# The w_out half of a squared-ReLU MLP: products carried through all of h in four passes, with the left-hand sums made a stage earlier

## The chip, the cores and the metric

The kernel runs on one core of a Trainium2 chip. The metric is the device time of one execution in microseconds (us). The engines are called as the profile calls them: PE (TensorE, matmuls; PEld its weight loads), DVE (VectorE), ACT (ScalarE), POOL (GpSimd) and SP (SyncE, which issues most DMAs).

## The reference

Two decoder layers over 1024 tokens of width 1024, in float32. Both end in the same kind of MLP, with a hidden width of 4096; the mixers and the shared K/V projection between the layers are not touched by the change.

```python
def sq_relu_mlp(h, w_in, w_out):
    return jnp.square(jax.nn.relu(h @ w_in)) @ w_out
...
for layer in range(DEPTH):
    ...                      # layer 0: RWKV-7 time mixing; layer 1: forgetting attention
    x = x + sq_relu_mlp(rmsnorm(x, mlp_norm_g[layer]), mlp_w_in[layer], mlp_w_out[layer])
    if layer == N_A_LAYERS - 1:
        k_sh, v_sh, c_sh = shared_kv(x, kv_norm_g, kv_w, kv_f_bias, k_norm_g)
```

## The kernel before, in words

Each layer's MLP has two stages. `mlp_in` (the w_in stage) computes h = relu(x w_in)^2 and stores it to DRAM; `mlp_out` (the w_out stage) loads it again and adds h w_out to the residual stream, which stays in SBUF as `xt`, eight tiles of 128 tokens by 1024.

Both stages multiply blocks of 2 by 2 quarters with seven products in place of eight. The left operands are four quarters or sums of them (A11, A12, A22, S1 = A21 + A22, S2 = S1 - A11, S3 = A11 - A21, S4 = A12 - S2), the right ones likewise (B11, B21, B22, T1 = B12 - B11, T2 = B22 - T1, T3 = B22 - B12, T4 = B21 - T2). Each result quarter is a sum of some products; U and V hold partial sums that several quarters share. The list SEVEN pairs them: (A11, B11), (A12, B21), (S2, T2), (S1, T1), (S3, T3), (A22, T4), (S4, B22).

Every operand is split into two parts of a reduced float32 type that PE takes at full rate (`split`): the high part is a cast, mostly on ACT (L700), the low part is source minus high part, a TENSOR_TENSOR on DVE or POOL (L703). A product of two split operands is three matmuls: high by high, high by low, low by high (L736 to L738 in w_in, L1329 to L1331 in w_out). A matmul here is 128x128 by 128x512.

`mlp_in` goes over 16 pairs of 128-column tiles of w_in (one tile from each half of the 4096 columns). A pair loads 1 MB of w_in, makes four sums of it on DVE (`form`, L1185), splits seven operands (`ah`, `al`; the low parts alternate between POOL and DVE), does seven products of twelve matmuls, and collects each with an add from PSUM on DVE (L1193). The four quarters of the pair's h get ReLU on ACT (L1195) and their square as a product on POOL (L1196). `z` holds h of a pair; two DMAs of 512 KB store it to `d_H`, on SP's queue, for the last pair on POOL's.

`mlp_out` calls `add_product`, which goes over the 4096 rows of w_out in four chunks. A chunk loads eight tiles of h and eight of w_out (tile `r`, 512 KB each), makes left-hand sums (S) and right-hand sums (T) on tiles of 128x512 by DVE and POOL, splits both sides (`oh`, `ol`), and does seven products of 48 matmuls, each into four PSUM banks. After each product of each chunk, DVE adds the banks to `xt` or to U (L1342); in the last chunk U is added to three quarters of `xt`, twelve of these adds on POOL (L1347). The result goes out on SP's queue (L1361): to `d_x` in layer 0, to `out` in layer 1.

Which engine an operation goes to is read from tables of letters (ENG, ENG_O). The order on each engine is set by a scheduler that simulates the program, with priority for some parts (`high_priority`); matmuls issued through `k.pe` and some loads are kept in program order. Memory is given out by pools whose order on the stack is a list of names, so a tile of one stage can wait for the last reader of a tile of the stage before.

## Time and profile before

| | us |
|---|---|
| three runs | 2941.09, 2938.45, 2939.36 (median 2939.36) |
| profiled execution | 2935.41 |
| its span | 2933.7, mean granted clock 0.947 |
| w_in, layer 0 | 890.6 to 1205.4 |
| w_out, layer 0 | 1205.4 to 1575.4 |
| w_in, layer 1 | 2250.3 to 2569.6 |
| w_out, layer 1 | 2569.6 to 2929.7 |

The stage borders are PE's: from the first matmul of a w_in stage to its last, from there to the last matmul of w_out. A few matmuls of layer 0's w_in (48 of 1344) stand before its row. "Granted clock" is the share of full speed that PE had. In groups of instructions a row reads: line, engine, operation, output and inputs, shapes, count, then busy time and mean ns of one, then the idle time of the engine just before them and what ended it. In a timeline a row has its start, its duration, and in brackets the idle time before it with its releaser.

### The profile page before, as it was taken

Reading aid. Unit: us, or ns where it says so; the run is one execution under the profiler, and the core shown is the slowest. Engines: PE = TensorE matmul, PEld = TensorE weight load, DVE = VectorE, ACT = ScalarE, POOL = GpSimd, SP = SyncE. Lnnn points to the kernel's source line nnn. Section 1 sums busy time; section 2 is a strip of 40 time slices with the busy share of each in tenths; the row PEclk is TensorE's granted clock in tenths of the full one; section 3 lists DMA queues with packets and bytes.
Section 4 is the critical chain, followed back from the end, with each engine's and each line's share of the span. In section 5 each row is a group of like instructions: output and inputs, shape, how many; then the busy total and the mean of one; then the engine's idle time right before and its main releaser. Section 6 shows DMA issues by size and latency. Waiting matters only on the chain.

```text
span 2933.7 us, 47183 instructions
## 1 busy us (share of the span) xinstructions
PE 2637.7 (90%) x17922; PEld 2183.9 (74%) x17922; DVE 2254.4 (77%) x3497; ACT 1191.8 (41%) x2245; POOL 1471.8 (50%) x1054
## 2 busy tenths in 40 slices
PE   7997788789998999889987899899986999989998
PEld 4776686677776888667766899888865888867876
DVE  7049998777768555699998878587789755599998
ACT  6364433432244333323334434487735333322432
POOL 3055553475546554566664422324266555466555
PEclk9998888899998999999998899999998999999999
DMA  3358574655412333532202232554330333442311
GB/s 116 141 180 247 159 210 137 176 164 145 116 50 72 115 111 105 201 115 100 73 11 92 72 102 75 164 148 134 95 123 13 97 114 108 143 159 86 115 58 58
DMA packets 330867, 344.66 MB, mean 117 GB/s; under 512 B 137392, under 2 KB 257440, under 8 KB 330640
## 3 DMA queue, kind: packets, MB, share of 16 engines
q1 hardware_dynamic: 329648, 339.48, 37.0%
q8 instruction: 141, 2.31, 0.3%
q0 software_dynamic: 992, 2.17, 0.2%
q14 instruction: 86, 0.70, 0.1%
HBM read 236.59 MB, written 104.99 MB: 116 GB/s over the span
## 4 chain that ended last, share of the span: by engine, by line
PE 50%; DVE 23%; issue 5%; DMA 3%; POOL 3%; ACT 1%; SPq 0%; DVEq 0%; POOLq 0%; ACTq 0%
PE mm L354 8%; PE mm L738 7%; PE mm L737 7%; PE mm L736 7%; DVE ol L703 5%; PE mm L1330 4%; PE mm L1331 4%; PE mm L1329 3%; DVE xt L1342 3%; PE wo L354 2%; PE tp L357 2%; PE o L354 1%; DVE Tm L301 1%; PE s L354 1%; DVE Tb L303 1%
## 5 line engine op out<-in xcount | busy, mean ns | idle before, releaser
L1330 PE MATMUL mm<-ol,oh 128*128 128x512 f32 x992 | 402.3, 408 | 43.9 <-DVE ol L703 38.5
L1331 PE MATMUL mm<-oh,ol 128*128 128x512 f32 x992 | 385.3, 405 | 16.1 <-DVE ol L703 15.7
L1329 PE MATMUL mm<-oh 128*128 128x512 f32 x992 | 365.7, 401 | 29.3 <-ACT oh L700 20.4
L1330 PEld LDWEIGHTS mm<-ol,oh 128*128 128x128 f32 x992 | 194.9, 197 | 100.5 <-DVE ol L703 52.6
L1329 PEld LDWEIGHTS mm<-oh 128*128 128x128 f32 x992 | 191.5, 194 | 76.6 <-ACT oh L700 23.2
L1196 POOL TENSOR_TENSOR z<-z 128x512 f32<-128x512 f32 x128 | 144.0, 1126 | 205.4 <-ACT z L1195 203.0
L1331 PEld LDWEIGHTS mm<-oh,ol 128*128 128x128 f32 x992 | 193.1, 196 | 63.3 <-DVE ol L703 23.2
L700 ACT CAST oh<-r 128x512 fp32r<-128x512 f32 x211 | 124.0, 619 | 250.1 <-PE mm L1330 192.8
L737 PE MATMUL mm<-xlT,ah 128*128 128x512 f32 x512 | 203.6, 398 | 17.1 <-DVE xlT L703 16.9
L736 PE MATMUL mm<-xhT,ah 128*128 128x512 f32 x512 | 202.1, 396 | 7.7 <-ACT xhT L700 5.5
L738 PE MATMUL mm<-xhT,al 128*128 128x512 f32 x512 | 202.0, 395 | 0.0
L703 DVE TENSOR_TENSOR ol<-r,oh 128x512 fp32r<-128x512 f32 x193 | 189.3, 1009 | 6.5 <-ACT oh L700 3.8
L1342 DVE TENSOR_TENSOR xt<-xt,mm 128x512 f32<-128x512 f32 x288 | 181.4, 675 | 7.0 <-PE mm L1331 6.9
L700 ACT CAST ah<-w 128x512 fp32r<-128x512 f32 x125 | 77.4, 621 | 182.5 <-PE mm L737 175.5
L703 POOL TENSOR_TENSOR ol<-r,oh 128x512 fp32r<-128x512 f32 x63 | 99.3, 1580 | 97.0 <-ACT oh L700 81.7
L738 PE MATMUL mm<-xhB,al 128*128 128x512 f32 x368 | 143.5, 391 | 1.0 <-DVE al L703 1.0
L737 PE MATMUL mm<-xlB,ah 128*128 128x512 f32 x368 | 144.1, 392 | 0.0
L736 PE MATMUL mm<-xhB,ah 128*128 128x512 f32 x368 | 143.9, 391 | 0.0
L700 ACT CAST oh<-S 128x512 fp32r<-128x512 f32 x102 | 63.0, 622 | 187.2 <-PE mm L1330 144.7
L737 PEld LDWEIGHTS mm<-xlT,ah 128*128 128x128 f32 x512 | 98.1, 192 | 41.4 <-DVE xlT L703 20.3
L703 DVE TENSOR_TENSOR ol<-S,oh 128x512 fp32r<-128x512 f32 x102 | 111.5, 1097 | 17.7 <-ACT oh L700 13.5
L703 POOL TENSOR_TENSOR ol<-T,oh 128x512 fp32r<-128x512 f32 x58 | 93.7, 1618 | 52.3 <-ACT oh L700 33.4
(527 smaller groups left out, 7794.5 us busy)
## 6 DMA issues: line engine op xcount, KB each, us to landing
w<-in_mlp_w_in_dram SPq DMA_DIRECT2D x64, 512.0 KB
r<-d_H SPq DMA_DIRECT2D x64, 512.0 KB
r<-in_mlp_w_out_dram SPq DMA_DIRECT2D x64, 512.0 KB
d_H<-z SPq DMA_DIRECT2D x60, 512.0 KB
raw<-in_rwkv_w_rkv_dram SPq DMA_DIRECT2D x24, 512.0 KB
d_KR<-KR SPq DMA_DIRECT2D x16, 512.0 KB
KRz<-d_KR SPq DMA_DIRECT2D x16, 512.0 KB
KRz<-d_BK SPq DMA_DIRECT2D x16, 512.0 KB
```

The lines of the kernel that those rows point to most:

```text
L354: return self.tc.keep_in_program_order(self.tc.nc.tensor.matmul(*args, **kw))
L357: return self.tc.keep_in_program_order(self.tc.nc.tensor.transpose(*args))
L700: nc.scalar.copy(hi, src)
L703: lo_eng.tensor_tensor(lo, src, hi.bitcast(F32), op=ALU.subtract)
L736: te.matmul(out, ah, bh, start=i == 0, stop=False)
L737: te.matmul(out, ah, bl, start=False, stop=False)
L738: te.matmul(out, al, bh, start=False, stop=i == n - 1)
L1196: nc.gpsimd.tensor_tensor(dst, dst, dst, op=ALU.mult)
L1329: te.matmul(banks[t], ah[:, ts], bh, start=i == 0, stop=False)
L1330: te.matmul(banks[t], ah[:, ts], bl, start=False, stop=False)
L1331: te.matmul(banks[t], al[:, ts], bh, start=False, stop=i == n - 1)
L1342: nc.vector.tensor_tensor(d, d, o, op=ALU.add)
```

## The change

`mlp_in`:

- The seven products of a pair come in another order (IN_ORDER), with A22 last.
- The square is made on ACT (Relu, then Square) instead of POOL. The low parts of w_in's operands are all on DVE (from the third pair on; before, every other one was on POOL).
- DVE makes the left-hand sums of h for w_out, four TENSOR_TENSORs of 128x512 a pair. S3 takes the place of C12 in `z`; S1, S2 and S4 go to new tiles `sums`.
- All seven left operands are stored: `d_H` has eight tiles of [128, 7, 2, 512], and a pair stores 7 x 256 KB in three DMAs on SP's queue, 29.4 MB a stage instead of 16.8.
- The split buffers go from four to three, and two operand pools change places in layer 1.

`mlp_out`:

- It goes over the 4096 rows four times, in passes of two products (the last of one): (A11, A12), (S2, S1), (S3, S4), (A22). A pass takes eight steps `q`; both products keep their four PSUM banks through all eight, and only then DVE adds them, 32 adds of 128x512 in a stage.
- A step loads its left operands ready made (`ra`, four buffers) and quarters of w_out (`rb`, six buffers, 256 rows of 512 columns, 2 KB each) on SP: 56 and 64 loads of 512 KB in a stage, 62.9 MB instead of 33.5.
- Right-hand sums and both parts of the split are made on tiles of 128x1024: high parts on ACT, low parts and sums on DVE. T2 is kept in SBUF for the last pass.
- POOL has twelve adds of U and V to `xt`, at the end of the second pass, and issues the stores of `d_x` and `out`.
- Matmuls are kept in program order. Their number stays 1344 a stage.

The K/V bias is loaded at the program's start, on POOL's queue.

The core of the diff:

```diff
--- before.py
+++ after.py
@@ -1145,6 +1147,11 @@
     return X
 
 
+IN_ORDER = ["A11", "A12", "S2", "S1", "S3", "S4", "A22"]
+
+LEFT = {n: i for i, n in enumerate(["A11", "S3", "A12", "A22", "S1", "S2", "S4"])}
+
+
 def mlp_in(k, a, l, xt, z, raw=None):
 
     nc, tc, ps = k.nc, k.tc, k.ps
@@ -1185,16 +1192,18 @@
                 engine(k, e).tensor_tensor(A[dst], A[x], A[y], op=op)
 
             def part(name, q, src=None):
-                S[name] = [wp.tile([P, NK // 2, P], F32R, tag=t, name=t, bufs=4) for t in ("ah", "al")]
-                es = [eng["wh"][7 * pr + q], eng["wl"][7 * pr + q]] if pr < 2 else ["s", "pv"[q % 2]]
+                S[name] = [wp.tile([P, NK // 2, P], F32R, tag=t, name=t, bufs=3) for t in ("ah", "al")]
+                es = [eng["wh"][7 * pr + q], eng["wl"][7 * pr + q]] if pr < 2 else ["s", "v"]
                 split(k, None, A[src or name], None, *(engine(k, e) for e in es), dst=S[name])
 
-            def add(dst, x, o, last=False):
+            def add(dst, x, o):
                 nc.vector.tensor_tensor(dst, x, o, op=ALU.add)
-                if last:
-                    nc.scalar.activation(dst, dst, AF.Relu)
-                    nc.gpsimd.tensor_tensor(dst, dst, dst, op=ALU.mult)
-            for q, (an, bn) in enumerate(SEVEN):
+
+            def square(x):
+                nc.scalar.activation(x, x, AF.Relu)
+                nc.scalar.activation(x, x, AF.Square)
+            for q, an in enumerate(IN_ORDER):
+                bn = dict(SEVEN)[an]
                 with tc.high_priority(offset=PRIO if pr == 0 or pr < AHEAD and q < 2 else 0):
                     if an == "S2":
                         A["S"] = wp.tile([P, NK // 2, P], F32, tag="S", name="S", bufs=1)
@@ -1221,21 +1230,33 @@
                     yield
                     Hs = z((pr + 1) % 2)
                     C11, C12, C21, C22 = Hs[:, 0, T1], Hs[:, 0, T2], Hs[:, 1, T1], Hs[:, 1, T2]
-                    add(C11, U, o, True)
+                    add(C11, U, o)
+                    square(C11)
                 elif an == "S2":
                     add(U, U, o)
                 elif an == "S1":
                     V = hp.tile([P, 512], F32, tag="V", name="V", bufs=1)
                     add(V, U, o)
                 elif an == "S3":
-                    add(C22, V, o, True)
+                    add(C22, V, o)
                     add(U, U, o)
-                elif an == "A22":
-                    add(C21, U, o, True)
+                    square(C22)
+                elif an == "S4":
+                    add(C12, V, o)
+                    square(C12)
+                    sums = [hp.tile([P, 2, 512], F32, tag="sums", name="sums") for _ in range(2)]
+                    (S1, S2), S4 = (sums[0][:, i] for i in range(2)), sums[1][:, 0]
+                    nc.vector.tensor_tensor(S1, C12, C22, op=ALU.add)
+                    nc.vector.tensor_tensor(S2, S1, C11, op=ALU.subtract)
+                    nc.vector.tensor_tensor(C12, C11, C12, op=ALU.subtract)
                 else:
-                    add(C12, V, o, True)
-            for h in range(2):
-                (nc.gpsimd if pr == F // 256 - 1 else nc.sync).dma_start(k.d_H[pr][:, h], Hs[:, h])
+                    add(C21, U, o)
+                    square(C21)
+                    nc.vector.tensor_tensor(S4, C21, S2, op=ALU.subtract)
+            dst = k.d_H[pr // 2][:, :, pr % 2]
+            nc.sync.dma_start(dst[:, 4:6], sums[0])
+            nc.sync.dma_start(dst[:, 0:4], Hs.rearrange("p h (f t) -> p (h f) t", t=512))
+            nc.sync.dma_start(dst[:, 6], S4)
         gens = [products(pr) for pr in range(F // 256)]
 
         def first_products(x):
@@ -1361,27 +1382,107 @@
                         nc.sync.dma_start(out[i * P:i * P + P, cols], d)
 
 
...
 def mlp_out(k, a, l, xt, out, norm):
 
-    nc, tc = k.nc, k.tc
+    nc, tc, ps = k.nc, k.tc, k.ps
+    w_out = a["mlp_w_out"][l]
+    D1, D2 = slice(0, 512), slice(512, 1024)
+    KP = F // 512
     with ExitStack() as ctx:
-        names = ("rb2-op-p-ra-rb1", "ra-op-p-rb1-rb2")[l].split("-")
+        names = ("k-ra-rb-op", "ra-rb-op-k")[l].split("-")
         p = {x: ctx.enter_context(tc.tile_pool(name="o_" + x, bufs=1, reuse_waits="tile")) for x in names}
-        raws = 0
-
-        def load(ap):
-            nonlocal raws
-            t = p[("ra", "rb1", "rb2")[raws % 24 // 8]].tile([P, 1024], F32, tag=f"r{raws % 24}", name=f"r{raws % 24}")
+        T2 = [p["k"].tile([P, 2, 512], F32, name=f"T2{i}") for i in range(KP)]
...
+        U, V = ([p["k"].tile([P, 512], F32, name=f"{n}{i}") for i in range(4)] for n in "UV")
+        SS = {}
+
+        def load(pool, n, ap):
+            t = p[pool].tile([P, 2, 512], F32, tag=pool, name=pool, bufs=n)
             with tc.high_priority(offset=PRIO):
                 tc.keep_in_program_order(nc.sync.dma_start(t, ap))
-            raws += 1
             return t
 
-        def tiles(c, h, i):
-            f = 4 * c + i
-            r0 = f * P + h * (F // 2)
-            return load(k.d_H[f][:, h]), load(a["mlp_w_out"][l][r0:r0 + P, :])
-        add_product(k, xt, F // P // 8, tiles, p["op"], p["p"], p["p"], out, norm, f"o{l}")
+        def left(name, q):
+            return load("ra", 4, k.d_H[q][:, LEFT[name]])
+
+        def right(name, q):
+            r0 = 256 * q + F // 2 * (name[1] == "2")
+            return load("rb", 6, w_out[r0:r0 + 256, (D1, D2)[int(name[2]) - 1]].rearrange("(j p) e -> p j e", p=P))
+
+        def parts(side, x):
+            h, lo = (p["op"].tile([P, 2, 512], F32R, tag=t + side, name="o" + t, bufs=3) for t in "hl")
+            return split(k, None, x, None, nc.scalar, nc.vector, dst=(h, lo))
+
+        def minus(dst, x, y):
+            nc.vector.tensor_tensor(dst, x, y, op=ALU.subtract)
+            return dst
+        quarter = {"11": lambda t: xt[t][:, D1], "12": lambda t: xt[t][:, D2],
+                   "21": lambda t: xt[t + 4][:, D1], "22": lambda t: xt[t + 4][:, D2]}
+        goes = {"A11": ["11"], "A12": ["11"], "S2": [], "S1": [], "S3": ["22", "21"], "S4": ["12"], "A22": ["21"]}
+        final = {"A12": "11", "S3": "22", "S4": "12", "A22": "21"}
+        for names in (("A11", "A12"), ("S2", "S1"), ("S3", "S4"), ("A22",)):
+            banks = {an: [ps.tile([P, 512], F32, tag="mm", name="mm") for _ in range(4)] for an in names}
+            for q in range(KP):
+                L = {an: left(an, q) for an in names}
+                if names[0] == "A11":
+                    R = {"A11": right("B11", q), "A12": right("B21", q)}
+                elif names[0] == "S2":
+                    b11, b12, b22 = (right(n, q) for n in ("B11", "B12", "B22"))
+                    t1 = minus(b12, b12, b11)
+                    R = {"S2": minus(T2[q], b22, t1), "S1": t1}
+                elif names[0] == "S3":
+                    b12, b22 = (right(n, q) for n in ("B12", "B22"))
+                    R = {"S3": minus(b12, b22, b12), "S4": b22}
+                else:
+                    b21 = right("B21", q)
+                    R = {"A22": minus(b21, b21, T2[q])}
+                for an in names:
+                    (ah, al), (bh, bl) = parts("a", L[an]), parts("b", R[an])
+                    bank = banks[an]
+                    end = an == "A22" and q == KP - 1
+                    for j, t in [(j, t) for t in range(4) for j in range(2)] if end else \
+                            [(j, t) for j in range(2) for t in range(4)]:
+                        ts = slice(t * P, t * P + P)
+                        k.pe.matmul(bank[t], ah[:, j, ts], bh[:, j], start=q == 0 and j == 0, stop=False)
+                        k.pe.matmul(bank[t], ah[:, j, ts], bl[:, j], start=False, stop=False)
+                        k.pe.matmul(bank[t], al[:, j, ts], bh[:, j], start=False, stop=q == KP - 1 and j == 1)
+                    if q < KP - 1:
+                        continue
+                    for t in range(4):
+                        if an == "A11":
+                            nc.scalar.copy(U[t], bank[t])
+                        elif an == "S2":
+                            with tc.high_priority(offset=PRIO):
+                                nc.vector.tensor_tensor(U[t], U[t], bank[t], op=ALU.add)
+                            d = quarter["21"](t)
+                            nc.gpsimd.tensor_tensor(d, d, U[t], op=ALU.add)
+                        elif an == "S1":
+                            with tc.high_priority(offset=PRIO):
+                                nc.vector.tensor_tensor(V[t], U[t], bank[t], op=ALU.add)
+                            for at in ("22", "12"):
+                                d = quarter[at](t)
+                                nc.gpsimd.tensor_tensor(d, d, V[t], op=ALU.add)
+                        for at in goes[an]:
+                            d = quarter[at](t)
+                            with tc.high_priority(offset=PRIO):
+                                nc.vector.tensor_tensor(d, d, bank[t], op=ALU.add)
+                            if final.get(an) == at:
+                                g, h = int(at[0]) - 1, int(at[1]) - 1
+                                if norm:
+                                    final_rows(k, p["k"], junk[t % 2], SS, t, g, h, d)
+                                if out is not None:
+                                    i = 4 * g + t
+                                    nc.gpsimd.dma_start(out[i * P:i * P + P, (D1, D2)[h]], d)
 
 
 def forget_gates(k, a, ps, pool, sp, X):
@@ -1788,7 +1888,7 @@
     nc.scalar.preload_act_table_set("natural_log_exp_and_others")
     k.rstd4 = [k.const.tile([P, 4], F32, name=f"rstd{i}") for i in range(2)]
     k.rstd = [k.rstd4[i // 4][:, i % 4:i % 4 + 1] for i in range(NK)]
-    k.d_H = [k.dram.tile([P, 2, T], F32, name=f"d_H{i}") for i in range(F // 256)]
+    k.d_H = [k.dram.tile([P, 7, 2, 512], F32, name=f"d_H{i}") for i in range(F // 512)]
     k.d_x = k.dram.tile([T, D], F32, name="d_x")
 
     def psum(stack):
```

On DVE, the end of w_in and the start of w_out in layer 0; `z`, `U`, `V` are quarters of h and partial sums, `al` and `ol` low parts, `r`, `ra` and `rb` loaded tiles. Before:

```order
L1193 TENSOR_TENSOR z<-V,mm 128x512
L1193 TENSOR_TENSOR U<-U,mm 128x512
L1193 TENSOR_TENSOR z<-U,mm 128x512
L1193 TENSOR_TENSOR z<-V,mm 128x512
L703 TENSOR_TENSOR ol<-r_11760,oh 128x512
L1297 TENSOR_TENSOR T<-r_11762 128x512
L703 TENSOR_TENSOR ol<-r_11762,oh 128x512
```

After:

```order
L1200 TENSOR_TENSOR z<-V,mm 128x512
L1200 TENSOR_TENSOR U<-U,mm 128x512
L1200 TENSOR_TENSOR z<-V,mm 128x512
L1249 TENSOR_TENSOR sums<-z 128x512
L1200 TENSOR_TENSOR z<-U,mm 128x512
L1250 TENSOR_TENSOR sums<-sums,z 128x512
L1251 TENSOR_TENSOR z<-z 128x512
L1255 TENSOR_TENSOR sums<-z,sums 128x512
L705 TENSOR_TENSOR ol<-ra,oh 128x1024 x2
L705 TENSOR_TENSOR ol<-rb,oh 128x1024 x2
```

The sums of the last pair now stand between its adds, and the first low parts of w_out come behind the last sum, on tiles twice as large.

On DVE, one of the last pairs of layer 0's w_in. Before:

```order
L1193 TENSOR_TENSOR z<-U,mm 128x512
L1185 TENSOR_TENSOR S<-S,w_11437 128x512
L1193 TENSOR_TENSOR z<-V,mm 128x512
L703 TENSOR_TENSOR al<-S,ah 128x512
L1185 TENSOR_TENSOR S<-w_11437,S 128x512
L1193 TENSOR_TENSOR z<-U,mm 128x512
L703 TENSOR_TENSOR al<-w_11439,ah 128x512
L1193 TENSOR_TENSOR U<-U,mm 128x512
```

After:

```order
L705 TENSOR_TENSOR al<-w_11685,ah 128x512
L1200 TENSOR_TENSOR z<-V,mm 128x512
L705 TENSOR_TENSOR al<-w_11685,ah 128x512
L1249 TENSOR_TENSOR sums<-z 128x512
L1200 TENSOR_TENSOR z<-U,mm 128x512
L1250 TENSOR_TENSOR sums<-sums,z 128x512
L1251 TENSOR_TENSOR z<-z 128x512
L705 TENSOR_TENSOR al<-S,ah 128x512
L1255 TENSOR_TENSOR sums<-z,sums 128x512
```

All low parts are now DVE's, and the four sums of h stand among them and the adds from PSUM.

On DVE, the change from the pass (S2, S1) to (S3, S4) in layer 0, where POOL's twelve adds begin; before it, the end of a product in the first chunk. Before:

```order
L703 TENSOR_TENSOR ol<-r_11786,oh 128x512
L1342 TENSOR_TENSOR U_11876<-U_11876,mm 128x512
L1342 TENSOR_TENSOR U_11877<-U_11877,mm 128x512
L1342 TENSOR_TENSOR U_11878<-U_11878,mm 128x512
L1342 TENSOR_TENSOR U_11879<-U_11879,mm 128x512
L703 TENSOR_TENSOR ol<-r_11760,oh 128x512
L703 TENSOR_TENSOR ol<-r_11762,oh 128x512
L702 CAST oh<-r_11766 128x512
```

After:

```order
L1466 TENSOR_TENSOR U_11873<-U_11873,mm 128x512
L1466 TENSOR_TENSOR U_11874<-U_11874,mm 128x512
L1466 TENSOR_TENSOR U_11875<-U_11875,mm 128x512
L1466 TENSOR_TENSOR U_11876<-U_11876,mm 128x512
L705 TENSOR_TENSOR ol<-ra,oh 128x1024
L705 TENSOR_TENSOR ol<-rb,oh 128x1024
L1471 TENSOR_TENSOR V_11877<-U_11873,mm 128x512
L1471 TENSOR_TENSOR V_11878<-U_11874,mm 128x512
L1471 TENSOR_TENSOR V_11879<-U_11875,mm 128x512
L1471 TENSOR_TENSOR V_11880<-U_11876,mm 128x512
L705 TENSOR_TENSOR ol<-ra,oh 128x1024
```

The four adds to U came between low parts; now the adds to U and to V, eight in all, stand together with only two low parts between them.

More of the change, by code (lines that the diff above doesn't have):

```diff
@@ L154, in load_cols @@
         return
+    k.f_bias = k.const.tile([H, 1], F32, name="f_bias")
+    nc.gpsimd.dma_start(k.f_bias, a["kv_f_bias"].rearrange("(h o) -> h o", o=1))
     def derive(name, src, mul, add):
@@ L1155, in mlp_in @@
         if l:
-            xp = operand_pools(k, ctx, "B11 B21 T2 T1 T3 T4 B22")
+            xp = operand_pools(k, ctx, "B11 B21 T2 T1 T3 B22 T4")
             wp = pool("m_w")
@@ L1256, in mlp_in @@
         x = operands(k, xp, ps, xt, k.col[f"mlp_norm_g{l}"], t3, normed, eng, first_products if early else None, None, raw,
-                 None if raw is None else hp.tile([P, D], F32, tag="junk", name="junk", bufs=1))
+                 None if raw is None else hp.tile([P, D], F32, tag="sums", name="junk"))
         X.update(x)
@@ L1361, in add_product, with final_rows @@
                         nc.sync.dma_start(out[i * P:i * P + P, cols], d)
+def final_rows(k, pool, junk, SS, t, g, h, d):
+    if g not in SS:
+        SS[g] = pool.tile([P, 2, 4], F32, name=f"SS{g}")
+    row_squares(k, d, junk, SS[g][:, h, t:t + 1])
+    SS[g, t] = SS.get((g, t), 0) + 1
+    if all(SS.get((g, i)) == 2 for i in range(4)):
+        rows_rstd(k, pool, SS[g], k.rstd4[g])
 def mlp_out(k, a, l, xt, out, norm):
-    nc, tc = k.nc, k.tc
+    nc, tc, ps = k.nc, k.tc, k.ps
+    w_out = a["mlp_w_out"][l]
+    D1, D2 = slice(0, 512), slice(512, 1024)
+    KP = F // 512
@@ L1375, in load @@
+        junk = [p["k"].tile([P, 512], F32, name=f"junk{i}") for i in range(2)]
+        U, V = ([p["k"].tile([P, 512], F32, name=f"{n}{i}") for i in range(4)] for n in "UV")
+        SS = {}
+        def load(pool, n, ap):
+            t = p[pool].tile([P, 2, 512], F32, tag=pool, name=pool, bufs=n)
             with tc.high_priority(offset=PRIO):
                 tc.keep_in_program_order(nc.sync.dma_start(t, ap))
-            raws += 1
             return t
-        def tiles(c, h, i):
-            f = 4 * c + i
-            r0 = f * P + h * (F // 2)
-            return load(k.d_H[f][:, h]), load(a["mlp_w_out"][l][r0:r0 + P, :])
@@ L1397, in forget_gates @@
     e_ = pool.tile([P, T], F32, tag="C", name="e_", bufs=3)[:H]
-    fb = sp.tile([H, 1], F32, tag="fb", name="fb")
-    nc.sync.dma_start(fb, a["kv_f_bias"].rearrange("(h o) -> h o", o=1))
+    fb = k.f_bias
     lo, hi = range(NK // 2), range(NK // 2, NK)
```

## The prediction

> **What bounds the kernel now.** I read the page first, then one row per stage, then the engines inside the changed stages. The page says that TensorE (PE) is busy 90% of the span, and DVE 77%.
>
> ```profile
> PE 2637.7 (90%) x17922; PEld 2183.9 (74%) x17922; DVE 2254.4 (77%) x3497; ACT 1191.8 (41%) x2245; POOL 1471.8 (50%) x1054
> ```
>
> An average hides stages, so here are the four that the change touches: w_in and w_out of layer 0, then of layer 1. Behind them stands a stretch inside w_in of layer 1, where PE never waits.
>
> ```profile
> core 0: us, PE busy (x) PEld busy (x) DVE busy (x) ACT busy (x) POOL busy (x), PEclk, DMA share, GB/s
> 890.60:1205.40 314.80, 305.10 (x1296) 246.55 (x1296) 191.12 (x239) 115.90 (x192) 166.01 (x134) 0.97 0.34 107
> 1205.40:1575.40 370.00, 329.09 (x1347) 261.42 (x1347) 341.72 (x407) 126.82 (x234) 228.62 (x151) 0.94 0.27 97
> 2250.30:2569.60 319.30, 307.89 (x1347) 253.32 (x1345) 198.10 (x248) 119.86 (x200) 171.95 (x136) 0.98 0.34 110
> 2569.60:2929.70 360.10, 326.57 (x1344) 258.08 (x1344) 339.08 (x419) 107.25 (x185) 219.29 (x148) 0.96 0.26 93
> 2300.00:2560.00 260.00, 260.00 (x1149) 215.36 (x1148) 150.30 (x193) 100.93 (x167) 135.80 (x111) 1.00 0.35 111
> ```
>
> The last row gives the pitch of a matmul at full clock: 260.0 / 1149 = 0.2263 us (I use 0.2268, as a few records can be missing). A w_out stage is 1344 matmuls, so 1344 x 0.2268 = 304.8 us if PE never waits. It takes 370.0 and 360.1: 65 and 55 us are lost there, while w_in loses 10 to 15. In w_out DVE is busy 341.7 of 370.0 and 339.1 of 360.1 us, so DVE sets the pace there. PE's own waits agree (w_out of layer 0; the last pair of numbers is idle time and who ended it):
>
> ```profile
> L1330 PE MATMUL mm<-ol,oh 128*128 128x512 f32 x448 | 183.2, 410 | 19.2 <-DVE ol L703 14.9 <-POOL ol L703 4.3
> L1331 PE MATMUL mm<-oh,ol 128*128 128x512 f32 x448 | 173.9, 404 | 8.7 <-DVE ol L703 8.7
> L1329 PE MATMUL mm<-oh 128*128 128x512 f32 x448 | 168.8, 404 | 13.0 <-ACT oh L700 12.0 <-DVE oh L702 0.8
> ```
>
> These are 41 us of waiting for the second ("low") parts of the split operands, and for casts; the rest is lost at a lower granted clock.
>
> **What DVE does in w_out, before and after.** Three groups carry its time in layer 0, and two rows elsewhere in the span price a low part and a cast on tiles twice as large, the size that the change uses:
>
> ```profile
> L703 DVE TENSOR_TENSOR ol<-r,oh 128x512 fp32r<-128x512 f32 x91 | 93.9, 1061 | 5.4 <-ACT oh L700 3.5 <-PE mm L1330 1.8
> L1342 DVE TENSOR_TENSOR xt<-xt,mm 128x512 f32<-128x512 f32 x126 | 79.5, 676 | 0.3 <-PE mm L1331 0.2
> L703 DVE TENSOR_TENSOR ol<-S,oh 128x512 fp32r<-128x512 f32 x46 | 49.4, 1078 | 13.9 <-ACT oh L700 11.1 <-PE mm L1330 2.1 <-POOL oh L702 0.5
> ...
> L703 DVE TENSOR_TENSOR wl<-S,wh 128x1024 fp32r<-128x1024 f32 x12 | 14.5, 1212 | 0.7 <-ACT wh L700 0.7
> L700 ACT CAST hi<-t 128x1024 fp32r<-128x1024 f32 x32 | 33.2, 1044 | 23.7 <-DVE t L886 22.0 <-PE mm L821 1.4
> ```
>
> After the change a stage has 7 products x 8 steps x 2 operands = 112 low parts of 128x1024 on DVE, at 1.21 us 136 us; 32 right-hand sums, also a TENSOR_TENSOR with both inputs in SBUF, 39 us; and 32 adds from PSUM at 0.676, 22 us. That is 197 us where there were 340: the partial products now stay in PSUM through all of h, and the left-hand sums are gone. ACT has 112 casts at 1.044 = 117 us, and 4 copies. POOL has 12 adds. No engine but PE is near the stage's length, so PE should set it. The gain can't exceed what the stage loses to PE today.
>
> **What stays lost in w_out.** Start: the first product needs the casts of both operands, and a low part. These are the rows of layer 0's start before (w_in's last matmul ends at 1205.4):
>
> ```profile
> 1205.46 0.69 DVE L1193 TENSOR_TENSOR z<-V,mm 128x512 f32<-128x512 f32 x1 [2.13 <-PE mm L738]
> 1206.18 0.63 ACT L1195 ACTIVATE z<-z 128x512 f32<-128x512 f32 x1 [2.18 <-DVE z L1193]
> 1208.40 4.72 DVE L1297 TENSOR_TENSOR T<-r 128x512 f32<-128x512 f32 x1
> 1208.85 1.29 POOL L1297 TENSOR_TENSOR T<-r 128x512 f32<-128x512 f32 x1
> 1210.09 1.26 POOL L703 TENSOR_TENSOR ol<-r,oh 128x512 fp32r<-128x512 f32 x1
> 1211.31 1.26 POOL L1297 TENSOR_TENSOR T<-r 128x512 f32<-128x512 f32 x1
> 1213.78 0.80 PE L1330 MATMUL mm<-ol,oh 128*128 128x512 f32 x1 [4.26 <-DVE ol L703]
> 2572.62 1.19 PE L1329 MATMUL mm<-oh 128*128 128x512 f32 x4 [3.02 <-DVE oh L702]
> ```
>
> After: the last add ends 0.8 us behind the last matmul, ReLU and square on ACT take 0.63 each, so ACT is free at 2.1; casts of two left tiles and the first right one end at 5.2. On DVE the low parts of the same three tiles end at about 6.7. So 6.7 us of gap, where it was 8.4 in layer 0 and 3.0 in layer 1. Behind it stands a low clock. These rows show its size:
>
> ```profile
> 1208.00:1212.00 4.00, 1.52 (x4) 0.70 (x4) 4.00 (x2) 2.44 (x5) 3.75 (x4) 0.56 0.99 401
> 1212.00:1216.00 4.00, 2.22 (x5) 1.84 (x6) 4.00 (x7) 0.00 (x0) 0.56 (x1) 0.50 1.03 420
> 1216.00:1220.00 4.00, 4.00 (x13) 3.15 (x12) 3.40 (x4) 0.00 (x0) 2.37 (x3) 0.66 1.01 406
> 2572.60:2576.60 4.00, 3.97 (x11) 2.87 (x12) 3.96 (x6) 0.00 (x0) 2.98 (x3) 0.65 0.94 364
> 2576.60:2580.60 4.00, 4.00 (x18) 3.29 (x17) 3.97 (x7) 0.92 (x2) 1.37 (x2) 0.93 1.02 419
> ```
>
> After 8.4 us of gap it is near half for about 10 us, a loss of 5; after 3.0 us it loses 4 x 0.35 + 4 x 0.07 = 1.7. For 6.7 us between them I take 4 (1.7 to 5).
>
> Pass changes: at the change from (S2, S1) to (S3, S4) POOL gets its 12 adds xt += U and xt += V in a row, while DVE has low parts to make and PSUM adds ahead of them. Their price, a stage before:
>
> ```profile
> L1347 POOL TENSOR_TENSOR xt<-xt,U 128x512 f32<-128x512 f32 x12 | 18.3, 1560 | 3.0 <-DVE U L1342 3.0
> ```
>
> That is 18.7 us of POOL. The nearest row for DVE beside it is the group of 91 low parts above, at 1.061 us with POOL busy 228.6 of 370.0 us. By that, a part of 128x512 costs 1.061 / 0.606 (half of 1.212) = 1.75 times its free price, so one of 128x1024 2.1 us and the four of a step 8.5, plus four PSUM adds, 2.7: 11.2 against the 10.9 us that PE takes for a step. With one product (5.4 us) prepared ahead that costs 0 to 2.5; with the other two pass changes, where only DVE's PSUM adds (four at 0.676) come ahead, I take 2.5 for the stage. The upper end is the row at 1208.40: one DVE operation took 4.72 us, through three POOL operations in a row. If DVE is held so through all 18.7 us, PE stops for 18.7 - 5.4 = 13 us. On this the Trainium skill (SBUF — State Buffer, section SBUF: two separate sides) says that DVE and GpSimd share a port pair as a lock held for the whole instruction, so the loser waits for one operation: about 1.3 us at 1208.40. The trace disagrees there, with three. By the rule the stage would stand at the lower value.
>
> The stage ends on its last four banks, in order of banks; its last add comes 0.7 us behind PE: 1 us. So a stage takes 304.8 + 6.7 + 4 + 2.5 + 1 = 319. It saves 51 in layer 0 and 41 in layer 1: 92 us.
>
> **Loads.** A stage loads 56 left and 64 right tiles of 512 KB, 62.9 MB, where it loaded 33.5; the densest pass (S2, S1) needs five in 10.9 us, 240 GB/s. The rows of 1208 to 1220 show 401 to 420 GB/s over 12 us, and w_in's share 0.34 at 107 GB/s stands for 315 at share 1. All lie above 240, so I cost the loads at nothing; the cover is the four and six buffers ahead of the splits.
>
> **w_in.** A pair is 84 matmuls, 19.05 us. Its DVE rows and ACT's casts in a steady stretch of layer 1, and POOL's square, now on ACT:
>
> ```profile
> L703 DVE TENSOR_TENSOR al<-w,ah 128x512 fp32r<-128x512 f32 x30 | 21.7, 724 | 0.0
> L1185 DVE TENSOR_TENSOR S<-S,w 128x512 f32<-128x512 f32 x15 | 21.3, 1418 | 15.5 <-POOL al L703 15.4
> L1193 DVE TENSOR_TENSOR z<-U,mm 128x512 f32<-128x512 f32 x30 | 20.6, 686 | 37.0 <-PE mm L738 37.0
> L700 ACT CAST ah<-w 128x512 fp32r<-128x512 f32 x56 | 34.8, 622 | 88.6 <-PE mm L737 88.6
> ...
> L1196 POOL TENSOR_TENSOR z<-z 128x512 f32<-128x512 f32 x128 | 144.0, 1126 | 205.4 <-ACT z L1195 203.0
> ```
>
> After, a pair has 7 adds (4.8 us), 7 low parts, 4 sums of w and 4 new sums of h on DVE: 15 operations with both inputs in SBUF. At 0.72 that is 4.8 + 10.8 = 15.6 of 19.05, hidden. The dearer price, 1418, stands where POOL works alongside; POOL now has nothing in steady w_in. At 1.42 a pair would take 26 us; DVE is the bound from (19.05 - 4.8) / 15 = 0.95 us. ACT's pair is 7 casts at 0.62, a copy, and 8 half-squares at 0.63: 10 us, hidden. The stores grow from four to seven times 256 KB on SP, under PE. So 0 for both w_in stages (-5 to +10): PE is full in their middle and can't get faster.
>
> **End and hand-over.** The stores of out and of d_x (layer 0's result) move from SP to POOL's queue. The rows: the span, the norm's scaling and PE's longest wait at layer 0's hand-over to the K/V projection, the last out stores, and a small POOL transfer.
>
> ```profile
> span 2933.7 us, 47183 instructions
> ...
> 1570.39 2.74 DVE L92 TENSOR_SCALAR hn<-xt,rstd 128x1024 f32<-128x1024 f32 x4
> 1590.36 0.58 PE L354 MATMUL mm<-wl,xhB 128*128 128x256 f32 x1 [7.04 <-DVE wl L703]
> 2927.78 3.05 SPq L1361 DMA_DIRECT2D out_dram<-xt  x4
> rows<-in_mlp_norm_g_dram POOLq DMA_DIRECT2D x2, 4.0 KB, 5.5
> ```
>
> On SP the last issue ends 2.9 us before the span's end (2933.7); a 4 KB POOL transfer takes 5.5 to land. I take +3 (0 to 6). At the hand-over the scaling (2.74, while w_out still runs to 1575.4) comes behind the last adds, and the weights' load waits for the last pass's operand memory, a 1 MB load or 2.6 us at 411 GB/s: up to +5. Four d_x stores, at 0.76 us an issue, leave SP's queue ahead of that load: down to -2. PE waits 7.04 us there for a split of the weights anyway, so most of it is hidden: +1. The K/V bias load is now issued at the program's start, 1500 us ahead of its use, and costs nothing.
>
> **Sum.** The profiled execution took 2935.4, 4.0 under the median of the runs (2939.36). 2935.4 - 92 + 3 + 1 = 2847; plus 4 against the median: 2851. With every unknown at its good end (stage 304.8 + 6.7 + 1.7 + 0.5 = 313.7, 103 saved, -5 in w_in, no tail) it would be 2827; no stall of PE at all gives 2820.
>
> **Rivals.** One: POOL holds DVE through its run of adds. PE stops 13 us and restarts at a lower clock (4) instead of the 2.5: some 14 more per stage, 2879. For it speaks 4.72 us at 1208.40; against it the mean of 1.061 over 91 operations beside a busy POOL.
>
> Two, slower: the loads bound w_out. It decides where 62.9 MB take as long as 319 + 46 = 365 us, so below 172 GB/s. The page's third line of slices goes as follows:
>
> ```profile
> GB/s 116 141 180 247 159 210 137 176 164 145 116 50 72 115 111 105 201 115 100 73 11 92 72 102 75 164 148 134 95 123 13 97 114 108 143 159 86 115 58 58
> ```
>
> At 159, a slice of the first third, a stage takes 396 and the kernel 2851 + 154 = 3005. Against it stand 247 over a slice of 73 us, and 401 to 420 in the rows above. The Trainium skill (DMA: Bandwidth & Descriptors, section Anatomy of one DMA — SWDGE (gpsimd) path) has a fit of 2.0 us plus bytes / 436e3 for each DMA; 120 loads one behind the other would then be 384 us, and the kernel, as an estimate by that page, 2981. The trace disagrees as far as several are in flight: at 411 GB/s one passes in 1.28 us.
>
> Three, slower: DVE becomes the bound of w_in, beyond 0.95 us an operation. It eats the whole gain from 1.14 us on ((19.05 + 92 / 32 - 4.8) / 15); at 1.42 the kernel is at 2851 + 32 x 7 = 3075. Against it: POOL has left the stage.
>
> Four: the change does nothing, since something other than DVE bounds w_out, about 2939. Against it speak 41 us of PE's waits that end on split operands.
>
> **How the numbers follow.** A measurement here can tell about 0.2%, 6 us, from no change. As forecast, 2835 to 2866: 0.58. Better, down to 2820: 0.12. The POOL rival, or as much lost at several pass changes, 2866 to 2900: 0.20. A gain of 6 to 39 us: 0.02. Nothing: 0.02. Loads bound: 0.03. DVE bounds w_in: 0.03. Faster 0.92, same 0.02, slower 0.06. The range 2824 to 2892 leaves out the slower cases and the edges, under 2 in 10.
>
> **What would show it.** In the new profile: w_out stages of 313 to 325 us, with DVE near 200; w_in at 312 to 320 with DVE's sums near 0.7 us; PE's longest idle in w_out at the stage's start, 6 to 8 us; the first product of (S3, S4) waiting under 3 us. I am wrong if PE waits there over 10 us, if the DMA share in (S2, S1) is at 1, or if w_in's DVE rows rise over 0.95 us.

## The result, and the profile after

The changed kernel takes 2847.11 us (median of four runs, 2844.21 to 2850.72) against 2938.9 before: ratio 0.9694, 95% interval 0.9671 to 0.9717. The forecast was 2851. Its profiled execution took 2847.68, with a span of 2845.9; all lines of before stem from a span of 2933.7.

The page of after, engines over the whole span:

```profile
PE 2605.9 (92%) x17922; PEld 2180.6 (77%) x17922; DVE 2071.9 (73%) x3275; ACT 1282.4 (45%) x2215; POOL 799.2 (28%) x575
```

The same four stages as before the change, from the kernel after:

```profile
core 0: us, PE busy (x) PEld busy (x) DVE busy (x) ACT busy (x) POOL busy (x), PEclk, DMA share, GB/s
892.20:1204.90 312.70, 304.06 (x1296) 246.82 (x1296) 235.71 (x358) 158.16 (x256) 21.57 (x14) 0.97 0.43 144
1204.90:1518.80 313.90, 308.17 (x1344) 254.28 (x1344) 199.93 (x185) 125.04 (x149) 32.00 (x27) 0.98 0.62 209
2201.70:2525.70 324.00, 310.22 (x1347) 254.48 (x1345) 244.35 (x367) 163.41 (x264) 24.25 (x17) 0.98 0.43 144
2525.70:2839.80 314.10, 308.28 (x1345) 254.28 (x1344) 198.88 (x180) 115.35 (x118) 31.96 (x27) 0.98 0.62 205
```

DVE's 341.7 and 339.1 us in w_out became 199.9 and 198.9, and POOL's 228.6 became 32.0. The two w_out stages lost 56 and 46 us. The rest of the span, piece by piece:

| piece of the span | before | after | change |
|---|---|---|---|
| up to w_in, layer 0 | 890.6 | 892.2 | +1.6 |
| w_in, layer 0 | 314.8 | 312.7 | -2.1 |
| w_out, layer 0 | 370.0 | 313.9 | -56.1 |
| hand-over: end of w_out, K/V and query projections, first scores | 323.4 | 330.4 | +7.0 |
| from there to w_in, layer 1 | 351.5 | 352.5 | +1.0 |
| w_in, layer 1 | 319.3 | 324.0 | +4.7 |
| w_out, layer 1 | 360.1 | 314.1 | -46.0 |
| last matmul to the end of the span | 4.0 | 6.1 | +2.1 |

The hand-over's row ends with the first 16 score matmuls (`s<-K,Q`), some 14 us behind the last matmul of the projections. The sum is -87.8, the difference of the spans. PE's waits in w_out of layer 0 were 41 us in three groups; now they are these:

```profile
L356 PE MATMUL mm<-ol,oh 128*128 128x512 f32 x448 | 175.7, 392 | 0.8 <-DVE ol L705 0.8
L356 PE MATMUL mm<-oh 128*128 128x512 f32 x448 | 175.6, 392 | 4.9 <-ACT oh L702 4.9
L356 PE MATMUL mm<-oh,ol 128*128 128x512 f32 x448 | 175.3, 391 | 0.0
```

Both waits are at the stage's start. Behind the second matmul PE never waits again in 300 us, not at a pass change either.

### The profile page after: what moved, and what is told of

It is laid out like the page before. It is cut to its first block, busy times and chain, and to the rows that moved or that the text cites. A ratio compares the mean times of both kernels' runs of the same rounds, so it can differ in the third digit from the quotient of the medians.

```text
span 2845.9 us, 46112 instructions
## 1 busy us (share of the span) xinstructions
PE 2605.9 (92%) x17922; PEld 2180.6 (77%) x17922; DVE 2071.9 (73%) x3275; ACT 1282.4 (45%) x2215; POOL 799.2 (28%) x575
## 5 line engine op out<-in xcount | busy, mean ns | idle before, releaser
L356 PE MATMUL mm<-ol,oh 128*128 128x512 f32 x896 | 351.3, 392 | 1.7 <-DVE ol L705 1.7
L356 PE MATMUL mm<-oh,ol 128*128 128x512 f32 x896 | 350.7, 391 | 0.0
L702 ACT CAST oh<-ra 128x1024 fp32r<-128x1024 f32 x112 | 117.8, 1054 | 354.7 <-PE mm L356 257.1
L705 DVE TENSOR_TENSOR ol<-ra,oh 128x1024 fp32r<-128x1024 f32 x112 | 142.7, 1276 | 140.5 <-ACT oh L702 140.3
L356 PEld LDWEIGHTS mm<-ol,oh 128*128 128x128 f32 x896 | 169.5, 189 | 38.3 <-DVE ol L705 2.7
L356 PEld LDWEIGHTS mm<-oh,ol 128*128 128x128 f32 x896 | 169.6, 189 | 35.2
L705 DVE TENSOR_TENSOR ol<-rb,oh 128x1024 fp32r<-128x1024 f32 x96 | 125.6, 1310 | 0.0
L738 PEld LDWEIGHTS mm<-xhT,ah 128*128 128x128 f32 x512 | 97.7, 191 | 35.3 <-ACT xhT L702 11.8
L356 PE MATMUL mm<-wl,xhT 128*128 128x256 f32 x384 | 111.2, 289 | 7.9 <-POOL wl L705 7.9
L356 PE MATMUL mm<-wh,xlT 128*128 128x256 f32 x384 | 111.7, 291 | 6.6 <-POOL xlT L705 6.6
```

The lines of the kernel that those rows point to most:

```text
L356: return self.tc.keep_in_program_order(self.tc.nc.tensor.matmul(*args, **kw))
L702: nc.scalar.copy(hi, src)
L705: lo_eng.tensor_tensor(lo, src, hi.bitcast(F32), op=ALU.subtract)
L738: te.matmul(out, ah, bh, start=i == 0, stop=False)
```

## The experiments

Each is one run with a profile unless its interval is given; the kernel before took 2933.78 and 2940.26 beside the first two groups of runs, so totals of single runs that differ by less than some 7 us are not told apart.

**DVE's work given back.** In the changed kernel's `parts`:

```diff
-            return split(k, None, x, None, nc.scalar, nc.vector, dst=(h, lo))
+            split(k, None, x, None, nc.scalar, nc.vector, dst=(h, lo))
+            nc.vector.tensor_tensor(lo, x, h.bitcast(F32), op=ALU.subtract)
+            return h, lo
```

> The changed kernel, but in w_out DVE makes every low part twice (the second time over the first), so DVE gets back 112 operations of 128x1024 a stage, some 130 us, and nothing else is different. Theory (the sum of DVE's work set the pace of w_out, and the gain is that it fell from 340 to 200 us): DVE comes to 200 + 130 = 330 us a stage, more than PE's 304.8, so both w_out stages grow from 314 to 335 to 350 us, and the kernel to 2890 to 2920 us. Rival (the gain came from fewer waits between chunks and from matmuls kept in order, not from DVE's sum): the stages stay under 320 and the kernel under 2860.

It took 2930.91, so the whole gain was gone: 21 us of the 102 are left in w_out, and the rest of the span takes 17 us more than before the change. The two w_out stages of this run:

```profile
1204.10:1556.90 352.80, 320.87 (x1344) 260.41 (x1344) 324.67 (x298) 125.76 (x150) 31.83 (x27) 0.94 0.56 186
2566.90:2923.00 356.10, 320.90 (x1344) 261.24 (x1344) 324.28 (x292) 115.69 (x118) 31.73 (x27) 0.94 0.54 181
```

DVE's sum sets the pace, as the theory had it; the pinned order of matmuls and the loads were left as they are and did not help. The stages came out 3 to 6 us above the range I gave, and the kernel 11 above its own: DVE's 325 us don't lie evenly. Of the 32 us that PE waits in layer 0's stage, 10.4 stand at its start (5.8 in the changed kernel) and 9.6 where POOL makes its twelve adds. Another 7.3 are waits inside the pass (S2, S1), whose two sums a step bring DVE to 10 x 1.14 = 11.4 us where PE takes 10.9, and 4.4 come later.

**POOL kept busy.** Behind `parts` in the changed kernel's w_out:

```diff
+                    for i in range(3):
+                        nc.gpsimd.tensor_tensor(spare, L[an][:, 0], L[an][:, 1], op=ALU.add)
```

> The changed kernel, but in w_out POOL does three idle adds of 128x512 for each product and step, 168 a stage, from the loaded left tile into a spare tile that nobody reads. Theory (a POOL operation and a DVE operation with both inputs in SBUF take turns, one at a time, as at the pass change of the changed kernel, where DVE's low parts went from 1.22 to 2.32 us and POOL's adds from 1.27 to 2.27): 144 x 1.22 + 180 x 1.27 = 405 us of turns, so stages near 400 and the kernel near 3020. Rival (DVE slows only by the mean factor of the kernel before, 1.75): 144 x 2.1 + 22 = 324, stages 325 to 335, the kernel near 2875. Third (POOL's runs hold DVE for several operations): over 450 a stage.

It took 2976.94, with stages of 379.6 and 374.8, nearest to the turns' 400. DVE and POOL in layer 0's w_out:

```profile
L705 DVE TENSOR_TENSOR ol<-ra,oh 128x1024 fp32r<-128x1024 f32 x56 | 115.1, 2057 | 16.6 <-ACT oh L702 16.6
L705 DVE TENSOR_TENSOR ol<-rb,oh 128x1024 fp32r<-128x1024 f32 x48 | 107.6, 2247 | 0.0
L1453 POOL TENSOR_TENSOR spare<-ra 128x512 f32<-128x512 f32 x162 | 318.7, 1967 | 13.1 <-DMA ra<-d_H 1.2
...
L1481 DVE TENSOR_TENSOR xt<-xt,mm 128x512 f32<-128x512 f32 x23 | 14.5, 676 | 10.5 <-PE mm L356 10.5
```

Low parts of 1.28 us take 2.06 to 2.25, POOL's adds of 1.27 take 1.97; adds that read PSUM stay at 0.68. With the step from one DVE operation to the next, 1.14, in place of its duration, the sum of turns is 144 x 1.14 + 174 x 1.27 = 385, and the stages took 380 and 375, 1 to 3% less. So it is about the sum of both engines' operations that sets the stage, though each engine alone would have had room (164 and 221 us).

**The kernel before, without POOL in w_out.** Its tables of engines:

```diff
+for _s in ("o0", "o1"):
+    ENG[_s] = {n: x.replace("p", "v") for n, x in ENG[_s].items()}
+ENG_O = {n: x.replace("p", "v") for n, x in ENG_O.items()}
```

> The kernel before, but all low parts, sums and casts that POOL did in w_out go to DVE (some 130 a stage; POOL keeps its 12 adds to xt). Theory (before, DVE's 342 us held about 107 us of waiting for POOL's turns): DVE alone is 224 x 0.61 + 154 x 0.60 + 8 = 237 us, and 130 x 0.61 = 79 more give 316, so the stages take no longer than 370 and 360, perhaps 340, and the kernel 2880 to 2940. Rival (DVE's 342 us are its own work): 342 + 130 x 0.68 = 430, stages 430 and 425, the kernel near 3060.

It took 2890.08, 44 us less than the kernel before, from a change of letters alone. Its w_out stages:

```profile
1209.90:1545.50 335.60, 316.09 (x1346) 256.74 (x1347) 328.07 (x539) 126.65 (x233) 21.90 (x16) 0.97 0.29 107
2541.90:2884.40 342.50, 320.99 (x1344) 258.12 (x1344) 334.19 (x552) 107.21 (x185) 21.59 (x15) 0.97 0.27 98
```

DVE has 132 instructions more than before and is busy 14 us less. Its own work was therefore about 328.1 - 132 x 0.61 = 248 us before, and by that some 94 of the 341.7 us that I read as DVE's work were waits for POOL. Of the 102 us that the change took out of w_out, 52 can be had by this edit to the old kernel.

**More loads.** One tile of 512 KB more for each product and step, read by nobody, through `load("op", 2, ...)`.

> The changed kernel, but each product and step loads one more tile of w_out, 512 KB that nobody reads: 92.3 MB a stage instead of 62.9. Theory (loads are hidden, with room): the pass (S2, S1) stood at a DMA share of 0.72 with five loads a step, so seven come to 1.0; the other passes stay under it. Stages 314 to 322, the kernel 2847 to 2865. Rival (loads are near what limits w_out): the stages grow with the bytes, to over 350, the kernel over 2920.

It took 2862.49; layer 0's w_out stayed at 314.0. This is the dense pass (S2, S1), with seven loads a step:

```profile
1300.00:1385.00 85.00, 85.00 (x376) 70.38 (x375) 58.97 (x54) 34.38 (x40) 4.92 (x6) 1.00 0.96 346
```

PE doesn't wait at a DMA share of 0.96. Layer 1's w_out took 322.0, since its first matmul came 13.7 us behind w_in instead of 4.9. Loads are hidden, with almost half as many again to spare; only the first ones count.

**Squares on POOL again.**

```diff
-                nc.scalar.activation(x, x, AF.Square)
+                nc.gpsimd.tensor_tensor(x, x, x, op=ALU.mult)
```

> The changed kernel, but the square of h goes back from ACT to POOL, four operations of 128x512 a pair beside DVE's 15 with both inputs in SBUF. Theory (turns: a POOL operation costs DVE at most its own 1.0 to 1.1 us): 22 DVE operations at 0.61 to 0.62 are 13.6 us a pair, 4 x 1.1 more make 18.0, under PE's 19.05, so the steady pairs stay and w_in grows by 0 to 10 us a stage, at its ends; the kernel 2847 to 2867. Rival (every DVE operation pays 1.42 us when POOL works in the stage): 26 us a pair, w_in 110 us longer, the kernel near 3070.

It took 2866.84, at the upper edge. The steady part of w_in didn't change: here PE is busy for all of 250 us.

```profile
950.00:1200.00 250.00, 250.00 (x1086) 202.33 (x1084) 188.97 (x284) 95.95 (x155) 65.80 (x52) 1.00 0.45 143
```

But w_in took 321.2 and 335.1 in all, 8.5 and 11.1 more, lost in the first 58 us, where DVE builds the right-hand operands: PE is busy there for 45.3 us instead of 49.2 in layer 0. The squares on ACT are worth about 20 us there in both layers together, and nothing in the middle.

**The hand-over.** Layer 0's pools in the order "op-k-ra-rb".

> The changed kernel, with layer 0's w_out pools stacked in the order op, k, ra, rb instead of k, ra, rb, op, so that the K/V weights' load after it takes memory of loaded tiles, which are read some 5 us before the last matmul, and not of split operands, which PE reads to the end. Theory (the hand-over's 7 us came from that load, issued at 1518.87 behind the last matmul): the load goes out 3 to 6 us before the end of w_out, and the time from the end of w_out to the end of the K/V projection falls from 330 to 324 to 327 us. Rival (the norm's scaling behind the last adds, and DVE and POOL taking turns in the hand-over, set it): the load goes earlier and the 330 stay.

The load went out at 1508.97, 20 us before the end of w_out (1528.6) and not 3 to 6, and the hand-over took 325.0 us instead of 330.4. But this run doesn't tell the theory from its rival, as the new order moved the norm's scaling as well: it ran 13.2 us ahead of the end of w_out, where it runs 0.6 us behind it in the changed kernel. The 5.4 us belong to both together. The run as a whole took 2853.45, as the new order costs more at the stage's start, where the second matmul came 17.3 us behind w_in instead of 6.6. ACT's first cast shows it:

```profile
1218.96 1.04 ACT L702 CAST oh<-ra 128x1024 fp32r<-128x1024 f32 x1 [11.74 <-DMA d_H<-z]
```

**Stores on SP.** `nc.gpsimd.dma_start(out...)` to `nc.sync.dma_start(out...)` in `mlp_out`.

> The changed kernel, with the stores of d_x and out on SP's queue again instead of POOL's. Theory: the time from the last matmul to the end of the span falls from 6.1 to about 4 us, as before the change, and nothing else moves; the kernel 2 us faster. Rival: at the hand-over the stores sit ahead of the K/V weights' load on SP and cost more than the 2 us.

It took 2911.7, 65 us more. The theory was right on the tail alone (3.8 us), and the rival looked at the wrong place: the w_out stages grew to 345.4 and 347.2. SP's queue and PE at the first pass change, and a stretch ahead of the last one:

```profile
1297.52 2.36 SPq L1485 DMA_DIRECT2D d_x<-xt  x4
1299.97 0.40 SPq L1412 DMA_DIRECT2D ra<-d_H  x1
...
1312.38 0.80 PE L356 MATMUL mm<-oh 128*128 128x512 f32 x1 [13.58 <-ACT oh L702]
...
1470.00:1480.00 10.00, 10.00 (x46) 8.29 (x45) 4.34 (x4) 2.54 (x3) 0.00 (x0) 1.00 0.00 0
```

The four stores wait for the adds at the end of the pass, and the next pass's loads stand behind them in the queue. At the first change PE then waits 13.58 us. Ahead of the last one the DMA share is 0.00 while PE uses up what was loaded, and PE waits 10.64 us behind that. The store's move to POOL's queue, which I had priced at +3, is what keeps the passes fed while their loads are on SP.

**POOL out of the rest.** In the changed kernel, `"p"` to `"v"` in ENG for "m0", "m1", "q", "w", and for the low parts of the projections.

> The changed kernel, with the low parts, sums and casts that POOL still does around the MLPs' operands, in the K/V and query projection and the output projections, given to DVE. Theory (one turn of POOL takes 1.27 us of the pair's time, the same operation on DVE 0.61, so wherever DVE sets the pace POOL's help costs time): the start of w_in in layer 1 loses less (324 falls to 312 to 318), the hand-over and the projections gain some, the kernel 2815 to 2840. Rival (DVE is then overloaded at those places, where POOL took a third of the work): the same or slower, 2847 to 2880.

It took 2826.97, 20 us less than the changed kernel. Layer 1's w_in stage:

```profile
2190.20:2505.40 315.20, 307.80 (x1347) 253.19 (x1345) 238.07 (x382) 162.33 (x263) 0.00 (x0) 0.99 0.44 147
```

It falls from 324.0 to 315.2, the hand-over with the projections from 330.4 to 322.3. One place lost: w_in of layer 0 began at 900.1 instead of 892.2. There DVE waits for PE and ACT anyway (5.42 and 2.84 us in single waits), and POOL's help was real.

**The best version.** The same, with layer 0's first splits left on POOL, and the first pass's loads as left, right, left, right:

```diff
+ENG["m0"] = {n: x.replace("p", "v") if n in ("t4", "T1l", "T3l", "T4l", "B22l") else x for n, x in ENG["m0"].items()}
+for _s in ('m1', 'q', 'w'):
+    ENG[_s] = {n: x.replace("p", "v") for n, x in ENG[_s].items()}
...
-                L = {an: left(an, q) for an in names}
+                L, R = {}, {}
+                for an in names:
+                    L[an] = left(an, q)
+                    if names[0] == "A11":
+                        R[an] = right(dict(SEVEN)[an], q)
```

> The changed kernel, with POOL's low parts, sums and casts given to DVE in layer 1's operands, the K/V and query projection and the output projections, and in layer 0's operands only for the right-hand forms that are made after the stage has begun (its first splits stay on POOL, which has them done while DVE waits for PE); and with the first pass's loads of w_out in the order left, right, left, right. Theory: w_in of layer 0 begins at 892 again (900 with all of them on DVE) and keeps its 308 us; the first product's pair of tiles lands and is cast one tile earlier, so the second matmul of w_out comes 5.4 us behind w_in instead of 6.6. The kernel 2814 to 2824. Rival (the turns of POOL in layer 0's first splits cost as much as they save): 2824 to 2832.

It took 2815.89 (five runs, 2814.89 to 2820.34): ratio to the kernel before 0.9588, 95% interval 0.9574 to 0.9601. Against the changed kernel's interval (0.9671 to 0.9717) it is clearly faster. The second matmul of w_out came 5.4 us behind w_in, as expected, and w_in of layer 0 began at 889.6.

**The best version with other pools in layer 0.** The order "rb-k2-ra-op-k", with U, V and junk in k2.

> The same, with layer 0's w_out pools stacked rb, U V junk, ra, op, T2, so that its first tiles lie on memory that w_in leaves early and the K/V weights' load on the tiles of T2. Theory: the load goes out some 5 us before the end of w_out and the hand-over falls by 4 to 6 us; the start stays at 5 to 7 us: 4 to 6 us under the run without it. Rival: a first load or cast waits for a later reader of the memory below it, and the start grows by more than the hand-over saves.

It took 2816.55: no gain. The rival happened: w_out's second matmul came 12.8 us behind w_in instead of 5.4. Of the 4 to 6 us that the theory gave to the hand-over 1.1 came (320.8 instead of 321.9), though the load went out at 1481.17, 34 us before the end of w_out. The norm's scaling ran 3.1 us behind that end, where it runs 0.6 behind it without the new order. The load alone gains little here.

**The kernel before, without POOL in all these places.**

> The kernel before, with POOL's low parts, sums and casts given to DVE in w_out and in all the places of the run above, and w_in's low parts too; POOL keeps the squares. Theory: what the four passes themselves are worth is the difference to the changed kernel in the same dress: w_out 336 and 342 here against 313 there, 50 us; the kernel 2862 to 2880. Rival (the passes are worth little once POOL is out of DVE's way): under 2850.

It took 2853.89, a little under the range: 85 us less than before, without any of the four passes. Its w_out stages took 333.3 and 337.4, against 311.8 and 313.0 of the best version. So with POOL out of DVE's way the change (with the loads' order at the start of its passes) is worth 2853.9 - 2815.9 = 38 us: 46 in w_out, less 7.0 at the hand-over (314.9 against 321.9). The squares are still POOL's in this run, and what they cost in it was not separated. As it was first made, the change is worth little more than this edit of letters to the old kernel: 2847.11 against 2853.89.

## Why the prediction was right, point by point

- **What bounds w_out.** Right that DVE did, and that its sum after would be 197 us (199.9 measured). Incomplete: I took 340 us as DVE's own work. The run without POOL puts some 94 of it down to waits for POOL's turns, so the change gained in two ways, by less work on DVE and by taking POOL out.
- **PE sets the stage.** 319 forecast, 313.9 and 314.1 measured. The start was right: 6.7 forecast, 6.6 measured. The low clock behind it was over-sized, 4 us: the rows after it cover some 13 matmuls at half speed, 427 ns apart and not 227, a loss of 2.6. With the start that makes up the stage (304.8 + 6.6 + 2.6 = 314.0):

```profile
1210.00:1214.00 4.00, 3.16 (x7) 2.19 (x8) 4.00 (x5) 2.58 (x3) 0.00 (x0) 0.50 1.03 338
1214.00:1218.00 4.00, 4.00 (x12) 3.13 (x12) 0.78 (x1) 0.00 (x0) 0.00 (x0) 0.60 1.03 395
1218.00:1222.00 4.00, 4.00 (x20) 3.28 (x19) 1.46 (x2) 2.00 (x2) 0.00 (x0) 1.00 0.39 155
```

- **Pass changes.** 2.5 us forecast, none measured. The prices were about right, if low: these are all engines, then DVE and POOL, where POOL has its run of adds. PE is busy for all of 25 us, with DVE busy for 24.6. A low part takes 2.32 (2.1 forecast), six of POOL's adds 12.53 and its twelve 24 (18.7 forecast):

```profile
1385.00:1410.00 25.00, 25.00 (x112) 20.71 (x111) 24.58 (x16) 8.17 (x9) 21.79 (x11) 1.00 0.51 168
...
1392.10 2.32 DVE L705 TENSOR_TENSOR ol<-rb,oh 128x1024 fp32r<-128x1024 f32 x1
1394.35 2.32 DVE L1427 TENSOR_TENSOR rb<-rb 128x1024 f32<-128x1024 f32 x1
1396.59 2.31 DVE L705 TENSOR_TENSOR ol<-ra,oh 128x1024 fp32r<-128x1024 f32 x1
...
1389.77 12.53 POOL L1474 TENSOR_TENSOR xt<-xt,V 128x512 f32<-128x512 f32 x6
```

  A DVE operation waits for one POOL operation, about 1.1 us, and not for three. The rule of the Trainium skill that I weighed (SBUF — State Buffer, section SBUF: two separate sides: the loser waits for one whole instruction) agrees with these rows, and the first rival falls. The 4.72 us of the row before is the only DVE operation in the 13 traces that spans three of POOL's. It began while POOL issued a store (1208.22 to 1208.83), but what made it so long stays open.
- **Loads.** Right: nothing, and nothing even with almost half as many again. With seven loads in a step of 10.9 us, a load of 512 KB passed every 1.6 us. The fit of the Trainium skill (DMA: Bandwidth & Descriptors, section Anatomy of one DMA — SWDGE (gpsimd) path) is for a DMA issued from GpSimd, and these loads go out on SP's queue, so the prediction read it for the wrong path. By estimate it would give 3.2 us for each, one behind the other, and the runs don't test it for its own path.
- **w_in.** 0 forecast, -2.1 and +4.7 measured, inside the bound given, though layer 1's 324.0 lies above the 312 to 320 that I had named as the sign of being right. DVE's low parts and sums took 0.69 to 0.76 us, so the third rival falls. Layer 1's w_in loses at its start, where DVE and POOL build operands in turns (the run without POOL took 8.8 us off it); why the change added 4.7 there was not separated.
- **Hand-over.** The step that failed: +1 forecast, with a bound of +5, and +7.0 measured. I took the weights' load and the norm's scaling as hidden behind PE's wait for a split of the weights. They were not: that wait ended 23.8 us behind w_out instead of 14.9. The load is issued behind the last matmul, where it was 8.2 us ahead of it, and the scaling starts 0.6 us behind it, where it was 5.0 ahead:

```profile
1518.87 0.92 SPq L1535 DMA_DIRECT2D w<-in_kv_w_dram  x2
1519.48 2.73 DVE L92 TENSOR_SCALAR hn<-xt,rstd 128x1024 f32<-128x1024 f32 x4
1542.67 0.58 PE L356 MATMUL mm<-wl,xhB 128*128 128x256 f32 x1 [8.94 <-DVE wl L705]
```

  Both moved ahead gave 5.4 of the 7.0 us back; the load alone, with the scaling 2.5 us later, gave 1.1 (in the best version). So the load is not shown to be the cause, and how the 7.0 us divide between the two stays open. POOL's work here, given to DVE, took 8 us off the kernel before and the changed one alike (323.4 to 314.9, 330.4 to 322.3), so it doesn't explain the difference.
- **Tail.** +3 forecast, +2.1 measured. What the move of the stores is worth I had not priced: 65 us, by the run with them on SP.

For the profiled execution the sum was 2847, and 2847.68 was measured. That closeness is luck: w_out came out 10 us better than its terms, and the rest, forecast at +4, at +14. The 4 us that I added for the median of before had no counterpart after (median 2847.11).

## What to carry to other kernels

Read DVE's and POOL's time as one sum where both run operations with two inputs in SBUF: they took turns here, so DVE's busy time held a quarter of waiting, and 132 operations moved from POOL to DVE made the kernel 44 us faster; POOL helped only where DVE was idle. Price such a change against the old kernel with its engines balanced anew, or the rebalancing is counted as the change's own gain. When a pass structure puts a store behind the end of a pass, look at which queue it blocks before pricing it by its own time. A stage whose loads are far ahead still pays for its first tiles: its start (gap and low clock, 9 us here) is what is left once its middle is bound by PE. An edit to the order of memory pools moves more than the one load it is meant for, so look at what else moved before giving it the gain.

## What the runs showed of the hardware that was not expected

- Turns were strict: at the pass change a DVE low part of 1.22 us and a POOL add of 1.27 us became 2.32 and 2.27, one after the other; DVE adds with one input in PSUM stayed at 0.68 with POOL busy 349 of 380 us. A DVE cast from SBUF, with one input, was held too: 0.41 us alone (1542.53 in the changed kernel), 2.56 beside a POOL sum of 128x1024 (1537.25).
- The DMA engines carried 346 GB/s at a share of 0.96 for 85 us, with rows of 2 KB and 4 KB, without one wait on PE.
